# Attention scores taken two levels at a time, a third factor buffer, and a longer stretch of other work behind the state products

## The chip, the cores and the metric

The kernel runs on one NeuronCore of a Trainium2 chip as one program. Its time is the device time of one execution in microseconds (us), lower is better. The names of the engines follow the profile: PE is TensorE (matmuls), PEld its loading of weights, DVE is VectorE, ACT ScalarE, POOL GpSimd, and SP the engine that issues most of the DMAs.

## What is computed

The kernel computes one layer of a hybrid encoder for 1024 tokens of width 1024 with 16 meta tokens ahead of them: a projection, a pooling mixer, a chunked gated linear attention, gates that merge the two, an output projection, and a squared-ReLU MLP. The change lies in the linear attention. For each of 4 heads (64 key and 128 value channels) and each chunk of 64 tokens:

```python
def gla_chunk_step(S, inp):
    qc, kc, vc, ac = inp
    b = jnp.cumsum(ac, axis=2)
    decay = jnp.exp(-jnp.abs(b[:, :, :, None, :] - b[:, :, None, :, :]))
    scores = jnp.einsum('bhtk,bhsk,bhtsk->bhts', qc, kc, decay)
    o = jnp.einsum('bhts,bhsv->bhtv', scores, vc) + jnp.einsum('bhtk,bhkv->bhtv', qc * jnp.exp(b), S)
    b_end = b[:, :, -1:, :]
    S_new = jnp.exp(b_end[:, :, 0, :])[..., None] * S + jnp.einsum('bhsk,bhsv->bhkv', kc * jnp.exp(b_end - b), vc)
    return S_new, o
```

`scores` has a decay of its own for every pair of tokens and channel, so it is no plain product of q and k. The state `S` passes from chunk to chunk.

## The kernel before

Everything is float32, and the large products are done as three matmuls on operands split in a high and a low part (`mm3`, lines 256 to 258). These three lines are by far the most of PE's work. The order of PE is fixed: it executes in the order in which the program is written (`manual_schedule` around the whole drive of the program). On DVE and ACT a scheduler in the build settles the order in the attention stage, out of the order of writing, what each instruction needs, and its own estimates; the engines then execute that order one instruction after the other. Which instruction waits for which is settled by what it reads and writes.

**The attention stage** (`gla`) works through four units: a unit is a pair of heads `p` and a half of the tokens, in the order (0,0), (1,0), (0,1), (1,1). A unit has two generators. `inside(p, half, before)` makes the scores within the chunks; `across(p, half)` handles the state and the output, and runs beside the `inside` of the next unit. In each round of the loop in `gla`, each living generator advances to its next `yield`. Then `pour` issues other work ("filler") on PE: matmuls of the key, value, gate and output projections, which wait in the list `fill`. The number of a `yield` is the length of the stretch to be poured, in us by the kernel's own reckoning, times `PACE` 1.1; the largest of a round counts. What is over or under in one pour is settled in the next. The list `fill` is a fixed amount of work: what isn't poured in a round is poured later.

**`inside`** gets the decays `g` from a small matmul (L1192) and a chain of ACT and DVE operations that ends with an exponential (L1263). Then the scores are built up over a hierarchy. Seven products are taken per unit by `scores`, each a block of 64x64 matmuls (L1249) into one half of the PSUM tile `sc`; the halves take turns. The first block is of plain keys and queries, copied to `scc` by ACT (L1266). The others, levels 0 to 5, use factors in which keys and queries are multiplied by decays, and a masked copy on DVE (L1312) takes from each level the pairs of tokens that belong to it. `grow` makes the factors of the next level from those of this one: DVE multiplies the outer quarters into the new buffer (L1281), ACT copies the inner ones there from the buffer `F` (L1282), DVE multiplies the inner ones in `F` (L1283), and DVE makes the products of decays for the next level, `ends` (L1285). There are two factor buffers, `n0` and `n1`, used by turns. So the factors of a level can only be written when the score block of two levels before has been read. Level 5 is made by `last` (L1294, L1295, L1296), which gives the operands of the state, `kl` and `qe`.

**`across`** transposes `kl` (L1330), takes the products of keys and values (L1338) into the PSUM tile `m2`, and runs the chain of states: eight DVE operations (L1344), each of which needs the one before. Behind a pour of 4.4 come the products of scores and values (L1351), which overwrite the PSUM tile that the chain reads; then a copy of a few elements, `seen` (L1356), after which the products of queries and states (L1361) may add to the same PSUM columns; then the norm of the output (L1370 to L1375), a transposition (L1379), a gate and the split of the result (`yg`, L1386 to L1393).

The rounds of a unit in the steady part are: decays; transposes with the plain score block; L1338 with level 0; L1351 with level 1; L1361 with level 2; then level 3, and L1379 with it or a round later; levels 4 and 5.

The products of weights for the filler are loaded by SP, split by ACT (L83) and by POOL (L87 in this stage), and the filler's results leave PSUM through ACT (L932 to L934, L1074) and DVE (L935, L962, L1157, L1158). `b_mm` and `b_mx` are the three PSUM banks of the filler, used by turns.

Of the kernel before, what the change touches and what calls it, by code (L numbers as in the profile page):

```python
# [8 lines left out]
F32 = mybir.dt.float32  # L9
F32R = mybir.dt.float32r  # L10
U8 = mybir.dt.uint8
ACT = mybir.ActivationFunctionType
ALU = mybir.AluOpType
AX = mybir.AxisListType

P = 128
# [4 lines left out]
HALF = 512  # L21
CH = 64
# [10 lines left out]
PACE, LEVEL = 1.1, 1.6  # L33
# [81 lines left out]
def kernel(  # L115
# [11 lines left out]
    left, right = Stack(tc, "left"), Stack(tc, "right")  # L127
# [895 lines left out]
    def gla_open():  # L1023
        W1.eng = pool
        right.pop_to(1)
        S["N"] = [left.push(f"n{i}", [P, HALF, 2], F32) for i in range(2)]
        S["F"] = left.push("f", [P, HALF, 2], F32)
        banks(keep=1, sc=1, m2=1, mx=1, ms=1)
        rota["mm"] = ("mm", "mm", "mx")
# [12 lines left out]

    def yg_open():
        right.pop_to(0)
        S["yg"] = {h: right.push(f"yg{h}", [P, 2, HEADS, HALF], F32R) for h in (1, 0)}
# [206 lines left out]
    def inside(p, half, before):  # L1252
# [4 lines left out]

        kq = S["kq"][half][:, p, :, OFF[half] : OFF[half] + HALF]
        N, F, scc, g, ends = S["N"], S["F"], S["scc"][:, p], S["g"], S["ends"]
        log_decay(S["lr"], p, HALF, g, S["y"], g)  # L1260
        if (p, half) == (1, 0):
            lr_of(1)
        act.activation(g, g, ACT.Exp, scale=1.0 / TAU)  # L1263
        yield 4.5
        b = scores(kq[:, 0], kq[:, 1])
        act.activation(scc, b, ACT.Copy)  # L1266
        pairs = lambda a: a.rearrange("p (b u) n -> p b u n", u=2)
# [31 lines left out]
        e, at = g, 0  # L1299
        for lvl in range(6):  # L1300
            m, n = 1 << lvl, N[lvl % 2]
            to = at + HALF // (2 * m)
            e2 = ends[:, at:to]
            if lvl < 5:
                grow(m, n, N[1 - lvl % 2], e, e2)
            else:
                while before and before not in done:
                    yield 0.8
                last(n, e, e2)
            e, at = e2, to  # L1310
            b = scores(n[:, :, 0], n[:, :, 1])
            dve.copy_predicated(scc, mask[:, lvl : lvl + 1, None, :].broadcast_to([P, 2, 4, CH]), b)  # L1312
            yield LEVEL

# [4 lines left out]
    def across(p, half):  # L1319
# [23 lines left out]
        for c, dst in enumerate(states[1:]):  # L1343
            dve.scalar_tensor_tensor(dst, states[c], dec[:, c : c + 1], kv[:, c % 2, c // 2], ALU.mult, ALU.add)  # L1344
        yield 4.4

# [8 lines left out]

        dve.tensor_copy(seen, o[:, :, 3, P - 1])  # L1356
        yield 0.8
# [495 lines left out]
```

## Time and profile before

| | |
|---|---|
| runs | 1212.27, 1213.29 and 4245.53 us; the median is 1213.29 us |
| the profiled execution | 1212.85 us, of which its span, from the first to the last instruction, is 1211.0 us |
| PE, share of the span | 98% |
| DVE, share of the span | 72% |
| ACT, share of the span | 51% |
| the attention stage | from about 304 to 470 us of the span |
| granted clock of PE | 0.998 |

One of the three runs is far from the other two; the profiled execution is near those two. "Busy" is the time in which an engine had at least one instruction in work. An instruction group shows its count, its mean duration and the idle time of its engine ahead of it with what ended that idle time. A row of the timeline shows when an instruction started, its duration, and in square brackets the wait ahead of it. On PE matmuls overlap, so the price of a block is read from the starts of the rows around it and not from its duration. A "x32" of the timeline is a block of 16 matmuls of the program, which the profile counts as two each.

### The profile page before, as it was taken

What the parts mean: (1) busy time and instruction counts of PE and PEld (TensorE: products, weight loads), DVE (VectorE), ACT (ScalarE), POOL (GpSimd) and SP (SyncE); (2) the same over time, 40 slices, a digit from 0 to 9 for tenths busy, and PEclk for the clock granted to TensorE, in tenths of its full rate; (3) what the DMA queues carried; (4) which work ended last, traced back from release to release, by engine and by line L of the source; (5) the groups of instructions that cost most, each with busy time, mean ns of one, the idle gap of its engine ahead of it and who ended that gap; (6) DMA issues with size and microseconds to landing.
All of it is one profiled execution on the core that took longest, in us unless ns stands there. A gap on an engine that the chain in (4) does not pass through costs nothing.

```text
span 1211.0 us, 18406 instructions
## 1 busy us (share of the span) xinstructions
PE 1191.4 (98%) x6794; PEld 992.8 (82%) x6794; DVE 874.3 (72%) x1442; ACT 623.3 (51%) x1115; POOL 60.3 (5%) x98
## 2 busy tenths in 40 slices
PE   7999999999999999999999999999999999999997
PEld 7878888898887877888878888888888888888886
DVE  7996677666667878636886767677675887887786
ACT  7667567744546423315655545455454444444554
POOL 2000000000103226000000000000000000000000
PEclk9999999999999999999999999999999999999999
DMA  9043433545107665922254444444479973333532
GB/s 256 2 113 114 121 94 102 154 125 159 40 20 258 196 206 196 327 89 88 87 158 164 152 143 156 146 161 149 153 251 322 348 226 97 98 99 92 174 96 87
DMA packets 144554, 182.24 MB, mean 150 GB/s; under 512 B 10264, under 2 KB 81712, under 8 KB 143952
## 3 DMA queue, kind: packets, MB, share of 16 engines
q1 hardware_dynamic: 143856, 176.81, 45.3%
q0 software_dynamic: 608, 4.26, 1.0%
q8 instruction: 53, 0.87, 0.3%
q14 instruction: 37, 0.30, 0.1%
HBM read 123.36 MB, written 57.67 MB: 149 GB/s over the span
## 4 chain that ended last, share of the span: by engine, by line
PE 87%; DVE 7%; ACT 3%; issue 1%; DMA 1%; POOL 0%; SPq 0%; DVEq 0%; ACTq 0%; POOLq 0%
PE b_mm L256 10%; PE b_mm L258 10%; PE b_mm L257 10%; PE b_ms L257 9%; PE b_ms L258 9%; PE b_ms L256 9%; PE b_x L257 8%; PE b_x L256 8%; PE b_x L258 8%; PE b_sc L1249 1%; PE b_mx L256 1%; PE b_mx L258 1%; PE b_mx L257 1%; DVE w1l L275 1%; DVE ut L787 1%
## 5 line engine op out<-in xcount | busy, mean ns | idle before, releaser
L256 PE MATMUL b_mm<-th,w1h 128*128 128x512 f32 (+1 forms) x308 | 116.2, 377 | 2.0 <-DVE c L822 1.0
L258 PE MATMUL b_mm<-th,w1l 128*128 128x512 f32 (+1 forms) x308 | 114.2, 371 | 0.0
L257 PE MATMUL b_mm<-tl,w1h 128*128 128x512 f32 (+1 forms) x308 | 114.2, 371 | 0.0
L256 PE MATMUL b_x<-th,w1h 128*128 128x512 f32 (+1 forms) x264 | 100.2, 379 | 0.0
L257 PE MATMUL b_x<-tl,w1h 128*128 128x512 f32 (+1 forms) x264 | 100.1, 379 | 0.0
L258 PE MATMUL b_x<-th,w1l 128*128 128x512 f32 (+1 forms) x264 | 99.7, 378 | 0.0
L274 ACT ACTIVATE w1h<-raw 128x512 fp32r<-128x512 f32 x98 | 60.7, 620 | 28.1 <-PE b_ms L257 13.6
L274 ACT ACTIVATE w1h<-fs 128x512 fp32r<-128x512 f32 x78 | 49.0, 630 | 48.1 <-PE b_ms L257 33.9
L275 DVE TENSOR_TENSOR w1l<-raw,w1h 128x512 fp32r<-128x512 f32 x98 | 67.0, 684 | 8.4 <-ACT w1h L274 8.4
L256 PEld LDWEIGHTS b_mm<-th,w1h 128*128 128x128 f32 x308 | 57.8, 188 | 13.6 <-issue 1.9
L258 PEld LDWEIGHTS b_mm<-th,w1l 128*128 128x128 f32 x308 | 57.9, 188 | 10.2
L257 PEld LDWEIGHTS b_mm<-tl,w1h 128*128 128x128 f32 x308 | 57.8, 188 | 9.3
L275 DVE TENSOR_TENSOR w1l<-fs,w1h 128x512 fp32r<-128x512 f32 x78 | 53.3, 686 | 16.3 <-ACT w1h L274 16.2
L274 ACT ACTIVATE w1h<-bt 128x512 fp32r<-128x512 f32 x44 | 27.8, 632 | 66.5 <-issue 62.2
L258 PEld LDWEIGHTS b_x<-th,w1l 128*128 128x128 f32 x264 | 49.7, 188 | 9.5
L256 PEld LDWEIGHTS b_x<-th,w1h 128*128 128x128 f32 x264 | 49.6, 188 | 9.5
L257 PEld LDWEIGHTS b_x<-tl,w1h 128*128 128x128 f32 x264 | 49.6, 188 | 9.2
L1701 DVE TENSOR_TENSOR bt<-w,w 128x512 f32<-128x512 f32 x80 | 54.7, 684 | 2.1 <-DMA w<-in_w_ff_dram 2.1
L274 ACT ACTIVATE fxh<-bt 128x512 fp32r<-128x512 f32 x36 | 22.8, 632 | 56.3 <-issue 50.6
L274 ACT ACTIVATE w1h<-rawx 128x512 fp32r<-128x512 f32 x44 | 27.5, 628 | 45.0 <-PE b_x L257 18.7
L258 PE MATMUL b_ms<-wo,w1l 128*128 128x512 f32 x128 | 49.9, 390 | 0.0
L256 PE MATMUL b_ms<-wo,w1h 128*128 128x512 f32 x128 | 49.8, 389 | 0.0
(447 smaller groups left out, 3331.8 us busy)
## 6 DMA issues: line engine op xcount, KB each, us to landing
hf_dram<-h SPq DMA_DIRECT2D x112, 256.0 KB, 2.1
raw<-hf_dram SPq DMA_DIRECT2D x112, 256.0 KB, 2.7
w<-in_w_ff_dram SPq DMA_DIRECT2D x64, 256.0 KB, 4.7
raw<-in_w_in_dram SPq DMA_DIRECT2D x22, 512.0 KB, 4.3
raw<-in_w_ff_dram SPq DMA_DIRECT2D x16, 512.0 KB, 4.2
rawx<-in_w_ff_dram SPq DMA_DIRECT2D x16, 512.0 KB, 4.1
rawx<-in_w_in_dram SPq DMA_DIRECT2D x10, 512.0 KB, 4.3
xs<-in_x_dram SPq DMA_DIRECT2D x8, 512.0 KB, 5.5
```

Source lines behind the costliest of these rows:

```text
L256: pe.matmul(ps, ah, bh, start=first and i == 0, stop=False, skip_group_check=more)
L257: pe.matmul(ps, ah, bl, start=False, stop=False, skip_group_check=more)
L258: pe.matmul(ps, al, bh, start=False, stop=last and i == n - 1, skip_group_check=more)
L274: act.activation(hi, a, ACT.Copy)
L275: dve.tensor_tensor(lo, a, f32(hi), ALU.subtract)
L787: dve.tensor_tensor(to_, a_, b_, ALU.subtract)
L1249: pe.matmul(b[to, e, j], kk[r, s], qq[r, s], start=True, stop=True, tile_position=(e * CH, u * CH))
L1701: dve.tensor_tensor(bt, w, S["w2"][q[3:]][:, i], ALU.add if q[2] == "+" else ALU.subtract)
```

## The change

Three things change in the attention stage; nothing is computed otherwise.

1. **Pairs of levels and a third factor buffer.** The factors rotate over three buffers. In the first unit the third is a new tile `n2`; in later units it lies over the keys and queries of the first unit, `kq0`, which are no longer needed. The seven score blocks of a unit are issued as (plain, level 0), (level 1, level 2), (level 3, level 4) and (level 5), with the two blocks of a pair directly behind each other on PE. The factors of level 1 are made before the first pair's blocks are written, those of level 2 behind them; those of levels 3 and 4 behind the second pair; those of level 5 behind the third. The plain block moves from the round of the transposes to that of the products of keys and values.
2. **Order on DVE.** The making of the factors of levels 3 and 4 is ordered behind the last operation of the chain of states. In the built order, the chain now stands together, with one masked copy in it.
3. **`across`.** The pour behind the chain of states is 5.4 instead of 4.4, except for the last unit. The copy `seen` goes from DVE to ACT.

```diff
--- before.py
+++ after.py
@@ -1,4 +1,4 @@
-from contextlib import ExitStack
+from contextlib import ExitStack, nullcontext
 from itertools import chain
 
 import concourse.bass as bass
@@ -1025,6 +1025,8 @@
         right.pop_to(1)
         S["N"] = [left.push(f"n{i}", [P, HALF, 2], F32) for i in range(2)]
         S["F"] = left.push("f", [P, HALF, 2], F32)
+        S["left_n2"] = left.mark()
+        S["N"].append(left.push("n2", [P, HALF, 2], F32))
         banks(keep=1, sc=1, m2=1, mx=1, ms=1)
         rota["mm"] = ("mm", "mm", "mx")
 
@@ -1041,6 +1043,8 @@
             leave()
 
     def yg_open():
+        assert S["unit"] != (0, 0)
+        left.pop_to(S["left_n2"])
         right.pop_to(0)
         S["yg"] = {h: right.push(f"yg{h}", [P, 2, HEADS, HALF], F32R) for h in (1, 0)}
 
@@ -1256,14 +1260,15 @@
 
 
         kq = S["kq"][half][:, p, :, OFF[half] : OFF[half] + HALF]
+        S["unit"] = p, half
         N, F, scc, g, ends = S["N"], S["F"], S["scc"][:, p], S["g"], S["ends"]
+        if (p, half) != (0, 0):
+            N[2] = S["kq"][0][:, 0].rearrange("p a b -> p (a b)")[:, : 2 * HALF].rearrange("p (t n) -> p t n", n=2)
         log_decay(S["lr"], p, HALF, g, S["y"], g)
         if (p, half) == (1, 0):
             lr_of(1)
         act.activation(g, g, ACT.Exp, scale=1.0 / TAU)
         yield 4.5
-        b = scores(kq[:, 0], kq[:, 1])
-        act.activation(scc, b, ACT.Copy)
         pairs = lambda a: a.rearrange("p (b u) n -> p b u n", u=2)
         plain, gp = kq.rearrange("p n (b u) -> p b u n", u=2), g.rearrange("p (b u) -> p b u", u=2)
         for u, to, other in ((1, N[0], F), (0, F, N[0])):
@@ -1297,20 +1302,38 @@
 
         yield 2.0
         e, at = g, 0
-        for lvl in range(6):
-            m, n = 1 << lvl, N[lvl % 2]
-            to = at + HALF // (2 * m)
-            e2 = ends[:, at:to]
-            if lvl < 5:
-                grow(m, n, N[1 - lvl % 2], e, e2)
-            else:
+
+        def up(lvl):
+            nonlocal e, at
+            to = at + HALF // (2 << lvl)
+            (grow if lvl < 5 else last)(*level(lvl), e, ends[:, at:to])
+            e, at = ends[:, at:to], to
+
+        def level(lvl):
+            return (1 << lvl, N[lvl % 3], N[(lvl + 1) % 3]) if lvl < 5 else (N[lvl % 3],)
+
+        def masked(lvl, b):
+            dve.copy_predicated(scc, mask[:, lvl : lvl + 1, None, :].broadcast_to([P, 2, 4, CH]), b)
+
+        up(0)
+        for pair in ((None, 0), (1, 2), (3, 4), (5,)):
+            if pair == (5,):
                 while before and before not in done:
                     yield 0.8
-                last(n, e, e2)
-            e, at = e2, to
-            b = scores(n[:, :, 0], n[:, :, 1])
-            dve.copy_predicated(scc, mask[:, lvl : lvl + 1, None, :].broadcast_to([P, 2, 4, CH]), b)
-            yield LEVEL
+                up(5)
+            made = []
+            for lvl in pair:
+                n = kq.rearrange("p n t -> p t n") if lvl is None else N[lvl % 3]
+                made.append((lvl, scores(n[:, :, 0], n[:, :, 1])))
+            with tc.issue_after(S["chain"].ins) if "chain" in S and pair[-1] == 2 else nullcontext():
+                for lvl in {0: (1,), 2: (2, 3), 4: (4,)}.get(pair[-1], ()):
+                    up(lvl)
+            for lvl, b in made:
+                if lvl is None:
+                    act.activation(scc, b, ACT.Copy)
+                else:
+                    masked(lvl, b)
+            yield len(pair) * LEVEL
 
     rms = [tiny(8) for _ in range(2)]
     seen = tiny(2)
@@ -1341,8 +1364,10 @@
                 )
         states = [first] + [W[:, c] for c in range(NC - 1)] + ([S["S"][:, 1, p]] if half == 0 else [])
         for c, dst in enumerate(states[1:]):
-            dve.scalar_tensor_tensor(dst, states[c], dec[:, c : c + 1], kv[:, c % 2, c // 2], ALU.mult, ALU.add)
-        yield 4.4
+            S["chain"] = dve.scalar_tensor_tensor(
+                dst, states[c], dec[:, c : c + 1], kv[:, c % 2, c // 2], ALU.mult, ALU.add
+            )
+        yield 4.4 if (p, half) == (1, 1) else 5.4
 
         o = two("m2").rearrange("p e (j c) -> p e j c", j=4)
         for j in range(4):
@@ -1353,7 +1378,7 @@
                         tile_position=(u * CH, (u ^ e) * CH), skip_group_check=True,
                     )
 
-        dve.tensor_copy(seen, o[:, :, 3, P - 1])
+        act.activation(seen, o[:, :, 3, P - 1], ACT.Copy)
         yield 0.8
         for j in (3, 0, 1, 2):
             for e, u in ((0, 0), (1, 0), (1, 1), (0, 1)):
```

On PE in unit (0,1), before: the products of scores and values with the block of level 1 behind them, and filler around them (`b_m2` is the PSUM tile of the state and output products, `b_sc` that of the scores, `n1` a factor buffer).

```order
L258 MATMUL b_mm_3875<-th1_140,w1l_128 128x512
L1351 MATMUL b_m2_3888<-v1_2690,scc_2715 64x128 x16
L1249 MATMUL b_sc_2951<-n1_2847 64x64 x16
L256 MATMUL b_mx_3930<-th1_140,w1h_124 128x512
L257 MATMUL b_mx_3930<-tl1_144,w1h_124 128x512
```

The same place in the changed kernel; `kq0` is now the third factor buffer and holds level 2.

```order
L258 MATMUL b_mx_3900<-th1_140,w1l_128 128x512
L1376 MATMUL b_m2_3913<-v1_2690,scc_2715 64x128 x16
L1253 MATMUL b_sc_2976<-n1_2847 64x64 x16
L1253 MATMUL b_sc_2976<-kq0_2234 64x64 x16
L256 MATMUL b_mm_3976<-th1_140,w1h_124 128x512
```

The block of level 2 stood behind a stretch of filler and the products of queries and states; it now follows the block of level 1 directly.

On DVE in unit (0,1), before: the chain of states (`W`, at the end `S`), the masked copy of level 0 into `scc`, and the multiplications that make the factors of level 2 (`n0`, `f`), then two operations of the filler.

```order
L1344 SCALAR_TENSOR_TENSOR W_2723<-S_2719,ends_2706,b_m2_3806 128x128
L1344 SCALAR_TENSOR_TENSOR W_2723<-W_2723,ends_2706,b_m2_3806 128x128 x2
L1312 COPY_PREDICATED scc_2715<-mask_91,b_sc_2951 128x512
L1344 SCALAR_TENSOR_TENSOR W_2723<-W_2723,ends_2706,b_m2_3806 128x128
L1281 TENSOR_TENSOR n0_2843<-n1_2847,ends_2706 128x64x2x4
L1344 SCALAR_TENSOR_TENSOR W_2723<-W_2723,ends_2706,b_m2_3806 128x128
L1283 TENSOR_TENSOR f_2851<-n1_2847,ends_2706 128x64x8
L1344 SCALAR_TENSOR_TENSOR W_2723<-W_2723,ends_2706,b_m2_3806 128x128 x2
L1344 SCALAR_TENSOR_TENSOR S_2719<-W_2723,ends_2706,b_m2_3806 128x128
L1296 TENSOR_TENSOR ends_2706<-ends_2706 128x8
L935 SCALAR_TENSOR_TENSOR t1_2694<-b_mm_3763,t1_2694 128x512
```

In the changed kernel, the same place begins with the factors of level 2, which go to `kq0`; then the chain, then the factors of level 3 in `n0`.

```order
L1286 TENSOR_TENSOR kq0_2234<-n1_2847,ends_2706 128x64x2x4
L1290 TENSOR_TENSOR ends_2706<-ends_2706 128x128
L1288 TENSOR_TENSOR f_2851<-n1_2847,ends_2706 128x64x8
L1367 SCALAR_TENSOR_TENSOR W_2723<-S_2719,ends_2706,b_m2_3800 128x128
L1367 SCALAR_TENSOR_TENSOR W_2723<-W_2723,ends_2706,b_m2_3800 128x128 x6
L1316 COPY_PREDICATED scc_2715<-mask_91,b_sc_2976 128x512
L1367 SCALAR_TENSOR_TENSOR S_2719<-W_2723,ends_2706,b_m2_3800 128x128
L1286 TENSOR_TENSOR n0_2843<-kq0_2234,ends_2706 128x32x2x8
L1290 TENSOR_TENSOR ends_2706<-ends_2706 128x64
L1290 TENSOR_TENSOR ends_2706<-ends_2706 128x32
L1288 TENSOR_TENSOR f_2851<-kq0_2234,ends_2706 128x32x16
```

The two multiplications that stood in the midst of the chain now stand ahead of it, and those behind it are of the next level.

On ACT in unit (0,1), before: the last part of a filler's gate (`t1`, `o`), the copy of inner factors, the square of the output for its norm.

```order
L932 ACTIVATE t1_2694<-b_mm_3763 128x512
L933 ACTIVATE t1_2694<-t1_2694 128x512
L934 ACTIVATE t1_2694<-t1_2694 128x512
L1074 ACTIVATE o_2698<-t1_2694 128x512
L1282 ACTIVATE n1_2847<-f_2851 128x32x16
L1370 ACTIVATE mix_2702<-b_m2_3888 128x1024
```

In the changed kernel, the same place holds the copy `seen` (to `small`), which reads the output products in `b_m2`.

```order
L1287 ACTIVATE n0_2843<-f_2851 128x32x16
L933 ACTIVATE t1_2694<-t1_2694 128x512
L934 ACTIVATE t1_2694<-t1_2694 128x512
L1078 ACTIVATE o_2698<-t1_2694 128x512
L1381 ACTIVATE small_99<-b_m2_3913 128x2
L1287 ACTIVATE n1_2847<-f_2851 128x16x32
```

The copy stands behind the gate of the filler and ahead of two copies of factors.

## The prediction

> **What bounds the kernel now.** I read the busy shares first, then the stage that the change touches, then what PE waits for there, then single blocks.
>
> ```profile
> PE 1191.4 (98%) x6794; PEld 992.8 (82%) x6794; DVE 874.3 (72%) x1442; ACT 623.3 (51%) x1115; POOL 60.3 (5%) x98
> PE 87%; DVE 7%; ACT 3%; issue 1%; DMA 1%; POOL 0%; SPq 0%; DVEq 0%; ACTq 0%; POOLq 0%
> ```
>
> PE sets the time: it is busy 98% of the span, and 87% of the chain that ended last is PE. In the attention stage, by windows (columns: PE, PEld, DVE, ACT, POOL busy, granted clock, DMA share, GB/s) and by waits of PE:
>
> ```profile
> 300.00:470.00 170.00, 167.44 (x2012) 138.63 (x2011) 118.75 (x244) 76.85 (x137) 38.15 (x48) 1.00 0.47 159
> PE b_m L1351 <- DVE S L1344: 0.7, 1, 0.7
> PE b_sc L1249 <- DVE scc L1312: 0.7, 1, 0.7
> PE b_m L1351 <- DVE W L1344: 0.5, 1, 0.5
> PE b_m L1379 <- DVE mix L1375: 0.4, 1, 0.4
> PE b_mx L256 <- DVE t L1157: 0.2, 1, 0.2
> ```
>
> PE is idle for 2.56 of 170 us, at full clock; the named waits are 2.3 us for operations that the change moves and 0.2 us for L1157, which it does not. The built order is the same from the last unit's products on and before the stage, on PE, DVE and ACT. So two things can be gained: these waits, and time in which PE is "busy" with changing over between kinds of matmul.
>
> **The price of a change-over.** On PE, a score block alone in the filler (columns: start, duration, engine, line, operation, count):
>
> ```profile
> 317.15 0.40 PE L258 MATMUL b_mm<-th,w1l 128*128 128x512 f32 x1
> 317.48 0.71 PE L1249 MATMUL b_sc<-n 64*64 64x64 f32 x32
> 318.12 0.50 PE L256 MATMUL b_mm<-th,w1h 128*128 128x512 f32 x1
> 318.45 0.39 PE L257 MATMUL b_mm<-tl,w1h 128*128 128x512 f32 x1
> 318.68 0.39 PE L258 MATMUL b_mm<-th,w1l 128*128 128x512 f32 x1
> ```
>
> Undisturbed filler starts every 0.23 us (318.45 to 318.68). From 317.15 to 318.45 there are 1.30 us with two filler matmuls, 0.46. The block alone costs **0.84 us**. Behind a product that uses the same 64x64 tiles:
>
> ```profile
> 452.80 1.10 PE L1338 MATMUL b_m<-v,mix 64*64 64x128 f32 x32
> 453.83 0.50 PE L256 MATMUL b_mm<-yg,w1h 128*128 128x512 f32 x1
> ...
> 418.51 1.10 PE L1338 MATMUL b_m<-v,mix 64*64 64x128 f32 x32
> 419.43 0.66 PE L1249 MATMUL b_sc<-n 64*64 64x64 f32 x32
> 420.02 0.50 PE L256 MATMUL b_mm<-th,w1h 128*128 128x512 f32 x1
> ```
>
> The product alone holds the filler back by 1.03 us, with a block behind it by 1.51. The block costs **0.48 us** there. Behind the transposes, which use the whole array, it gains nothing:
>
> ```profile
> 450.18 0.60 PE L1330 MATMUL b_ms<-ident,mix 128*128 128x128 f32 x4
> 450.53 0.48 PE L256 MATMUL b_mm<-yg,w1h 128*128 128x512 f32 x1
> ...
> 375.96 0.60 PE L1330 MATMUL b_ms<-ident,mix 128*128 128x128 f32 x4
> 376.49 0.69 PE L1249 MATMUL b_sc<-kq 64*64 64x64 f32 x32
> 377.11 0.50 PE L256 MATMUL b_mm<-th,w1h 128*128 128x512 f32 x1
> ```
>
> 1.15 less 0.35 is 0.80 us, nearly the price of a block alone.
>
> **The change, part by part.** *Pairs.* Before, seven blocks of unit (0,0) stand alone, and in each later unit four: the plain one, level 3 (with the transposes L1379 or alone), 4 and 5. That is 19 at 0.84 and 9 at 0.48. After, unit (0,0) has four groups; in later units each of three pairs follows a 64x64 product, and level 5 follows the transposes. That leaves 4 + 3 = 7 blocks that pay the change-over, and 21 that don't. Twelve blocks, the second ones of the pairs, go from 0.84 to a lower price. No row shows a block behind another block. The lower bound of its price is 0.48, from the block behind a product; the upper is 0.64, the time from 317.48 to 318.12 that a lone block holds the filler back behind its own start. I take 0.48, since that row too is 64x64 behind 64x64. **12 x 0.36 = 4.3 us less**, or 12 x 0.20 = 2.4 with 0.64.
>
> [...]
>
> *Waits behind the chain of states.* On DVE in unit (0,1), where the wait of 0.7 us is:
>
> ```profile
> 377.39 0.69 DVE L1281 TENSOR_TENSOR n<-n,mix 128x512 f32<-128x512 f32 x1
> 377.99 0.97 DVE L1285 TENSOR_TENSOR ends<-mix 128x256 f32<-128x256 f32 x1
> 378.99 2.27 DVE L1285 TENSOR_TENSOR ends<-ends 128x128 f32<-128x128 f32 x4
> 381.17 0.68 DVE L935 SCALAR_TENSOR_TENSOR t<-b_mx,t 128x512 f32<-128x512 f32 x1
> 381.77 0.68 DVE L1283 TENSOR_TENSOR f<-n,mix 128x512 f32<-128x512 f32 x1
> 382.37 0.34 DVE L1344 SCALAR_TENSOR_TENSOR W<-S,ends,b_m 128x128 f32<-128x128 f32 x1
> 382.75 0.73 DVE L1344 SCALAR_TENSOR_TENSOR W<-W,ends,b_m 128x128 f32<-128x128 f32 x2
> 383.40 0.73 DVE L1312 COPY_PREDICATED scc<-mask,b_sc 128x512 f32<-128x512 uint8 x1
> 384.02 0.33 DVE L1344 SCALAR_TENSOR_TENSOR W<-W,ends,b_m 128x128 f32<-128x128 f32 x1
> 384.27 0.68 DVE L1281 TENSOR_TENSOR n<-n,ends 128x512 f32<-128x512 f32 x1
> ...
> 386.94 0.35 DVE L1344 SCALAR_TENSOR_TENSOR S<-W,ends,b_m 128x128 f32<-128x128 f32 x1
> ```
>
> The chain takes 4.9 us, from 382.37 to 387.29. Standing together it needs 8 x 0.38 (382.37 to 382.75) and one masked copy of 0.62 (383.40 to 384.02): 3.7 us. But two multiplications, 1.2 us at 0.6 from start to start (381.77 to 382.37), move ahead of it. Three of the small `ends` move behind it, at least 0.7 us. So it ends about 0.7 us earlier against the decays. In this unit ACT's order puts a load's split (L83, 1.05 us) ahead of the exponential that all this waits for, so the end may come 0.3 later instead. PE comes later to the products: the longer pour adds 1.1 us, two blocks at 0.48 stand where one stood, the plain block's 0.80 is gone ahead, and three filler matmuls (0.7) more stand ahead of the transposes. That is about 1.5 us. Both waits for the chain, 0.7 and 0.5, should go; what is next there is PE itself.
>
> *Waits for the norm and a masked copy*, 0.4 and 0.7, both in unit (1,1). In the rounds around L1375, two multiplications for factors and one or two operations of the filler no longer stand between the reduction (L1373) and L1375; one masked copy more does. The norm comes earlier by 2 x 0.6 - 0.62 = 0.6 us at least, and the level-4 block asked for earlier no longer waits there. I take all four waits as gone: **2.3 us less**; the bounds are nothing and 2.3.
>
> *What is now asked for earlier.* Level 2 is wanted a round earlier, level 4 two rounds. In unit (0,1) DVE has, from the end of the chain to the masked copy that frees the level-4 block's half of `sc`, five multiplications at 0.6, two masked copies at 0.62, four `ends` at about 0.2, and three filler operations at 0.6 (L935, 381.17 to 381.77): 6.8 us. PE needs 1.03 + 2 x 0.48 for the products and blocks, 3.5 for the pour, 1.03 and 0.48 until that block, 7.0 us, and the chain ends about a microsecond before it. The slack is a microsecond. Against it: where POOL is in work, these multiplications are slower.
>
> ```profile
> 414.91 3.99 POOL L87 TENSOR_TENSOR w1l<-raw,w1h 128x256 fp32r<-128x256 f32 x4 [11.47 <-ACT w1h L83]
> L1281 DVE TENSOR_TENSOR n<-n,mix x4: 673/686/1215, 311.7 to 416.2; 128x512 f32<-128x512 f32 x4
> ```
>
> The one of 1215 ns (minimum 673, median 686) started at 416.2, within POOL's 414.91 to 418.90: 0.53 us more. I add **0.6 us** of new waits, between nothing and 3 us (six such slow operations).
>
> *The copy `seen`* costs PE nothing unless it comes behind the pour. On ACT it stands behind a filler gate and ahead of two copies. After the pairs PE pours 3.5 us before it is needed; only in the last unit is the pour 0.9 us. A small operation on ACT takes 0.30 us:
>
> ```profile
> 394.71 0.30 ACT L220 ACTIVATE small<-small 128x8 f32<-128x8 f32 x1 [0.77 <-DVE small L1373]
> ```
>
> So it is hidden, with half a microsecond of slack in the last unit; if the cover is gone, it costs these 0.3 us a unit. *The filler* is the same in count, and the same work stands behind the last chain in both orders. The pours of a later unit sum to 4.5 + 2 + 5.4 + 3.2 + 6 + 1.6 = 22.7 against 23.3, so no unit is stretched. DMAs and the queues of SP and POOL change only in interleaving.
>
> **Sum.** 1212.85 (profiled execution) - 4.3 - 2.3 + 0.6 = 1206.9; with the rounding of rows, **1207 us**, half a per cent under the median of 1213.29. About 2% is what a measurement of this kernel can tell from no change, so this counts as no change.
>
> **The rivals.**
>
> *The second block of a pair costs nearly as much* (0.64), and half of the waits come back in other places: 1212.85 - 2.4 - 1.2 + 0.6 = 1209.9. For it: the lone block's own 0.64 is what is seen most. Against: the three places behind products show 0.48.
>
> *The waits hide other waits, and PE's order gains nothing*: the change does not do what it says, 1213. For it: PE is idle only 1.5% of the stage, and 98% busy all over. Against: the change-over is within busy time, and 0.36 us is measured.
>
> *Level 4 comes too late, and the time ends above before.* The place is the third pair in units (1,0), (0,1), (1,1). The ten multiplications of a unit up to there run while POOL splits weights; at 0.53 us each that is 5.3 us a unit, less a slack of 1 us in (0,1) and, as an estimate, 2.6 in each of the others, where the chain ends earlier or DVE has less of the filler: 3 x 5.3 - 6.2 = 9.7 us of waits, and 1212.85 - 6.6 + 9.7 = 1216. It decides from 6.6 us of new waits, 2.2 a unit. Against: POOL's block is 4 us long, so that few of the ten fall in one, and the unit in which it lies paid no more than the wait of 0.5 for the chain. [...]
>
> **How the numbers follow.** Forecast 64%, the dear second block 20%, no gain 6%, late level 4 10%. The forecast's own bounds are 1205.8 (all gains, no new wait) and 1209.5 (3 us of new waits); the second rival reaches to 1211. The range 1205.6 to 1212.0 leaves out the no-gain and the late case and little else. None of the cases comes near 2%, which is 24 us; 1% faster, 97% within, 2% slower is for stalls that no row here hints at.
>
> **What would show it.** The pairs on PE: the second block's start to the next filler at about 0.5. Idle of PE in the stage under 1 us, with no wait of L1376 (then the line of L1351) for the chain. DVE's chain in one piece of 3.7 us. Wrong would be: waits of the score blocks for `f`, `n` or `scc` in the third pair, a wait of L1386 for ACT's copy, or filler waiting for a bank because L935 is late.

## The result, and the profile after

The changed kernel takes **1205.88 us**, the median of six runs (1204.46 to 1206.74). The kernel before, measured with it, takes 1212.8 us, the median of six runs, or 1212.4 without the one run of 4245.53 us that stands far from the others. The ratio of the others is 0.9944, with a 95% interval from 0.9934 to 0.9954: nearly seven microseconds, half a per cent. The profiled execution is the slowest of the six, 1206.74 us, with a span of 1205.0 us.

The page of the changed kernel, engines and chain (the lines that answer to the first two of the prediction):

```profile
PE 1186.7 (98%) x6794; PEld 992.4 (82%) x6794; DVE 874.9 (73%) x1438; ACT 623.9 (52%) x1119; POOL 60.2 (5%) x98
PE 89%; DVE 5%; ACT 2%; DMA 2%; issue 1%; POOL 0%; SPq 0%; DVEq 0%; POOLq 0%; ACTq 0%
```

PE has the same 6794 instructions, and its busy time is 4.7 us less. The attention stage can be cut out exactly: it begins with the first matmul of the decays and ends with the first filler matmul behind it that goes to `b_x`; so it ends at 477.6 us in the kernel before, not at about 470. From the timeline and the windows of the kernel before:

```profile
304.21 0.17 PE L1192 MATMUL b_mm<-lrT_meta,wgu 80*128 80x16 f32 x1
477.58 0.39 PE L256 MATMUL b_x<-yg,w1h 128*128 128x512 f32 x1
304.21:477.58 173.37, 170.81 (x2029) 141.55 (x2028) 125.48 (x252) 78.83 (x141) 43.69 (x53) 1.00 0.48 159
```

The same stretch of the changed kernel:

```profile
304.66 0.17 PE L1196 MATMUL b_mm<-lrT_meta,wgu 80*128 80x16 f32 x1
472.08 0.39 PE L256 MATMUL b_x<-yg,w1h 128*128 128x512 f32 x1
304.66:472.08 167.42, 166.04 (x2029) 140.71 (x2028) 125.72 (x247) 79.37 (x144) 43.60 (x53) 1.00 0.50 165
```

In both windows PE has 2029 matmuls, so this is the same work. The stage is 5.95 us shorter: busy time fell by 4.77 us, from 170.81 to 166.04, and idle time by 1.18 us, from 2.56 to 1.38. The two profiled executions differ by 6.11 us (1212.85 to 1206.74), so nearly all of the gain lies in this stage.

What PE waits for in the stage of the changed kernel:

```profile
PE b_m L1386 <- ACT small L1381: 1.2, 1, 1.2
PE b_mx L256 <- DVE t L1161: 0.2, 1, 0.2
```

The four waits of before (0.7, 0.7, 0.5 and 0.4 us) are gone. There is one new wait, of the last unit's products of queries and states (L1386, formerly L1361) for the copy `seen` (L1381, formerly L1356).

A pair of blocks on PE, behind the products of keys and values of unit (0,1):

```profile
378.65 0.40 PE L258 MATMUL b_mm<-th,w1l 128*128 128x512 f32 x1
378.98 1.10 PE L1361 MATMUL b_m<-v,mix 64*64 64x128 f32 x32
379.90 0.64 PE L1253 MATMUL b_sc<-kq 64*64 64x64 f32 x32
380.37 0.66 PE L1253 MATMUL b_sc<-n 64*64 64x64 f32 x32
380.96 0.50 PE L256 MATMUL b_mm<-th,w1h 128*128 128x512 f32 x1
```

The product and two blocks hold the filler back by 1.98 us, from 378.98 to 380.96. Before, the product with one block took 1.51. The second block costs **0.47 us**, where a block alone cost 0.84.

The chain of states on DVE in the same unit:

```profile
382.27 0.34 DVE L1367 SCALAR_TENSOR_TENSOR W<-S,ends,b_m 128x128 f32<-128x128 f32 x1
382.64 2.27 DVE L1367 SCALAR_TENSOR_TENSOR W<-W,ends,b_m 128x128 f32<-128x128 f32 x6
384.82 0.74 DVE L1316 COPY_PREDICATED scc<-mask,b_sc 128x512 f32<-128x512 uint8 x1
385.45 0.33 DVE L1367 SCALAR_TENSOR_TENSOR S<-W,ends,b_m 128x128 f32<-128x128 f32 x1
387.32 1.10 PE L1376 MATMUL b_m<-v,scc 64*64 64x128 f32 x32
```

It stands in one piece with one masked copy in it, from 382.27 to 385.78, which is 3.5 us instead of 4.9. PE pours until 387.32, when L1376 (formerly L1351) starts: the chain is 1.5 us early.

**Where the new wait comes from.** From SP's issues to PE, in the last unit of the changed kernel (SPq rows: when a DMA was issued):

```profile
444.80 0.38 SPq L963 DMA_DIRECT2D ma_dram<-o  x1
451.64 0.79 SPq L1095 DMA_DIRECT2D o<-ma_dram  x2
454.48 0.69 DVE L1162 TENSOR_TENSOR t<-t,o 128x512 f32<-128x512 f32 x1 [0.52 <-DMA o<-ma_dram]
455.20 0.63 ACT L1165 ACTIVATE th<-t 128x512 fp32r<-128x512 f32 x1 [2.86 <-DVE t L1162]
455.74 0.15 ACT L1381 ACTIVATE small<-b_m 128x2 f32<-128x2 f32 x1
455.95 0.45 PE L1386 MATMUL b_m<-W,mix 64*64 64x128 f32 x8 [1.18 <-ACT small L1381]
```

The copy itself takes 0.15 us. Ahead of it on ACT stands the split of the merged results (L1165), which waits for DVE's sum (L1162), which waits for a load that was issued only at 451.64. SP had been held there:

```profile
SPq L1095 <- DMA ma_dram<-o: 7.6, 2, 4.5
```

The load goes into a slot of `o`, of which there are three. By this row SP waited until an earlier result had left its slot on the way to `ma_dram`.

### The profile page after: what moved, and what is told of

Read it like the earlier page. It is cut to its first block, busy times and chain, and to the rows that moved or that the text cites. A ratio compares the mean times of both kernels' runs of the same rounds, so it can differ in the third digit from the quotient of the medians.

```text
span 1205.0 us, 18370 instructions
## 1 busy us (share of the span) xinstructions
PE 1186.7 (98%) x6794; PEld 992.4 (82%) x6794; DVE 874.9 (73%) x1438; ACT 623.9 (52%) x1119; POOL 60.2 (5%) x98
## 4 chain that ended last, share of the span: by engine, by line
PE 89%; DVE 5%; ACT 2%; DMA 2%; issue 1%; POOL 0%; SPq 0%; DVEq 0%; POOLq 0%; ACTq 0%
PE b_mm L256 10%; PE b_mm L258 10%; PE b_mm L257 10%; PE b_ms L258 10%; PE b_ms L257 10%; PE b_ms L256 10%; PE b_x L257 8%; PE b_x L256 8%; PE b_x L258 8%; PE b_sc L1253 1%; PE b_mx L256 1%; DMA ma_dram<-o 1%; PE b_mx L258 1%; PE b_mx L257 1%; DVE ut L787 1%
```

## Experiments

The theory was the prediction's: blocks in pairs save 0.36 us each, and the longer pour and the order on DVE keep the waits away. The rivals were that the busy time went for another reason, that the waits would have gone without these parts, and, once the trace was seen, that the parts around the pairs work through the late load of the last unit. The ratios are to the kernel before, which was run beside each series and had medians of 1212.6 to 1212.9 us; where a time is set against the 1205.88 us of the changed kernel, that is across series.

### The pairs split up

```diff
             for lvl in pair:
+                if len(pair) > len(made):
+                    S["pour"](0.65)
...
-            yield len(pair) * LEVEL
+            yield len(pair) * LEVEL - 0.59 * (len(pair) - 1)
```

Three or six filler matmuls stand between the two blocks of each pair; the rest is the changed kernel.

> The changed kernel with one short stretch of filler (three or six matmuls) between the two blocks of each pair, taken from the pour behind the pair; everything else as changed. Theory (the gain is the change-over of PE between filler and 64x64 blocks): each of 12 second blocks costs 0.84 instead of 0.48 us, so 1205.9 + 4.3 = 1210.2 us, with PE's waits as in the changed kernel. Rival (the gain comes from the waits that went, or from the times at which factors are made): 1205.5 to 1206.5 us. Third, if a block drains the array whatever stands ahead of it: no change either, and the second blocks show the same price in both.

Measured: 1213.96 us (1213.49 to 1216.24), ratio to the kernel before 1.001, interval 1.0001 to 1.0019. All of the gain is gone. PE in unit (0,1), and the stage:

```profile
385.26 0.64 PE L1253 MATMUL b_sc<-kq 64*64 64x64 f32 x32
385.83 0.50 PE L256 MATMUL b_mm<-th,w1h 128*128 128x512 f32 x1
386.17 0.39 PE L257 MATMUL b_mm<-tl,w1h 128*128 128x512 f32 x1
386.39 0.40 PE L258 MATMUL b_mm<-th,w1l 128*128 128x512 f32 x1
386.72 0.71 PE L1253 MATMUL b_sc<-n 64*64 64x64 f32 x32
387.36 0.50 PE L256 MATMUL b_mm<-th,w1h 128*128 128x512 f32 x1
387.70 0.40 PE L257 MATMUL b_mm<-tl,w1h 128*128 128x512 f32 x1
304.82:478.87 174.05, 171.26 (x2029) 141.13 (x2028) 127.29 (x248) 79.83 (x145) 44.78 (x55) 1.00 0.48 158
```

From 386.39 to 387.70 there are 1.31 us with two filler matmuls of 0.23; the second block costs 0.85 us again, with only three filler matmuls in front of it. The same 2029 matmuls are busy for 171.26 us, 5.22 more than with the pairs. Idle time is 1.41 us more; one wait of 1.4 us for POOL's split (L87) is new and was not expected. So the busy time is the pairs', and the expectation of 1210.2 was too low: 12 pairs are worth 5.2 us here and 4.8 in the comparison with before, 0.40 to 0.44 us each, somewhat more than the 0.37 that the rows of one pair show.

### The copy `seen` back on DVE

```diff
-        act.activation(seen, o[:, :, 3, P - 1], ACT.Copy)
+        dve.tensor_copy(seen, o[:, :, 3, P - 1])
```

> The changed kernel with the copy `seen` back on DVE. In the changed profile L1386 waits 1.2 us for it in the last unit, and nowhere else. Theory A (ACT's queue is at fault: the copy stands behind another instruction there): the wait goes, 1204.7 us. Theory B (a load of the output merge lands late, and the DVE operation that needs it, L1162, stands ahead of the copy on DVE as well): a wait of 0.6 to 0.9 us stays, for DVE, and the time is 1205.2 to 1205.6 us.

Measured: 1205.36 us (1204.87 to 1206.82), ratio 0.9941, interval 0.9929 to 0.9953: not to be told from the changed kernel. The time lies in theory B's range, but the trace is theory A's: PE's wait at L1386 is gone from the stage, which leaves only the 0.2 us for L1161. In the MLP, PE waits 1.4 us in two places for DVE (L1664), where the profiled execution of the changed kernel has no such wait, and the spans are the same 1205.0 us. The part "`seen` on ACT" is worth nothing that these runs can tell.

### A longer pour in the last unit

```diff
-        yield 0.8
+        yield 2.2 if (p, half) == (1, 1) else 0.8
```

> The changed kernel with a pour of 2.2 instead of 0.8 between the copy `seen` and L1386, in the last unit alone. If the copy's lateness is all that holds PE there, six to seven filler matmuls cover the 1.2 us, and the time is 1204.7 us with no wait at L1386. Rival: the filler behind the norm is then short by as much, and the 1.2 us come back as a wait of L1404 or of the filler for its loads; 1205.9 us.

Measured: 1207.72 us (1205.72 to 1210.28), ratio 0.9959, interval 0.9946 to 0.9971; neither expected time held. The five runs are far apart, and the profiled execution, 1209.55 us, is one of the slower. In it the wait at L1386 went, and another came at the transposes of the output, the place that the rival named, with a lower clock behind it:

```profile
466.49 1.80 PE L1404 MATMUL b_m<-ident,mix 128*128 128x128 f32 x8 [2.26 <-DVE mix L1400]
464.00:468.00 4.00, 1.74 (x10) 1.51 (x9) 3.76 (x8) 0.21 (x1) 0.68 (x1) 0.84 0.64 201
468.00:472.00 4.00, 4.00 (x15) 3.24 (x14) 3.93 (x7) 2.29 (x4) 3.50 (x4) 0.73 0.37 79
```

The filler is a fixed amount: what is poured ahead of L1386 is missing ahead of L1404.

### The pairs alone, and the third part alone

The pairs alone: the changed kernel without the order on DVE, with the pour of 4.4 and `seen` on DVE.

```diff
-            with tc.issue_after(S["chain"].ins) if "chain" in S and pair[-1] == 2 else nullcontext():
+            with nullcontext():
...
-        yield 4.4 if (p, half) == (1, 1) else 5.4
+        yield 4.4
...
-        act.activation(seen, o[:, :, 3, P - 1], ACT.Copy)
+        dve.tensor_copy(seen, o[:, :, 3, P - 1])
```

> Only the pairs and the third buffer: no order behind the chain on DVE, pour 4.4, `seen` on DVE. Theory (pairs carry the change-over, the other two parts only the waits of L1376 for the chain): PE's blocks as in the changed kernel, the waits for the norm and the masked copy gone, but waits of up to 1 us in two or three units for the chain, so 1206 to 1208.5 us. Rival (order and pour are what makes the pairs possible): waits of several us for the chain and for factors, 1210 us or more.

Measured: 1211.81 us (1210.53 to 1212.73), ratio 0.999, interval 0.9981 to 0.9999. The time is in the rival's range: the pairs alone keep 1.1 of the seven microseconds. Two long waits of PE, and the clock behind the first and the second of them:

```profile
386.75 1.10 PE L1376 MATMUL b_m<-v,scc 64*64 64x128 f32 x32 [2.53 <-DVE S L1367]
388.00:392.00 4.00, 4.00 (x66) 3.40 (x60) 3.50 (x8) 1.47 (x3) 0.00 (x0) 0.60 0.90 295
457.62 0.45 PE L1386 MATMUL b_m<-W,mix 64*64 64x128 f32 x8 [2.56 <-DVE small L1381]
460.00:464.00 4.00, 4.00 (x19) 3.30 (x18) 3.30 (x8) 0.54 (x3) 0.00 (x0) 1.00 1.02 366
```

The stage takes 173.17 us, as long as before, of which PE is idle for 5.26 and busy for 167.91. What the pairs save, PE now waits: it comes to the same DVE results earlier.

The third part alone, on the kernel before (the second, the order on DVE, was not tried there):

```diff
-        yield 4.4
+        yield 4.4 if (p, half) == (1, 1) else 5.4
...
-        dve.tensor_copy(seen, o[:, :, 3, P - 1])
+        act.activation(seen, o[:, :, 3, P - 1], ACT.Copy)
```

> The kernel before with the third part alone: pour 5.4 behind the chain of states, `seen` on ACT; two buffers, no pairs. Theory (pour removes only the two waits of L1351 for the chain, 0.7 and 0.5): 1211.5 to 1212.0 us, those two waits gone, the waits for the norm and the masked copy as before or moved, perhaps 1 us for `seen` in the last unit, then 1212.5 us. Rival (the longer pour is what won the 7 us): 1207 to 1209 us.

Measured: 1217.16 us (1215.55 to 1217.43), ratio 1.0031, interval 1.0019 to 1.0044: slower, outside both expectations. Its waits in the stage:

```profile
PE b_m L1361 <- ACT small L1356: 2.5, 1, 2.5
PE b_sc L1249 <- DVE scc L1312: 1.5, 2, 0.8
```

The two waits for the chain went, as the theory has it. But PE waits 2.5 us for the copy in the last unit: on ACT it stands behind a split of weights (L83) that waits 3.79 us for its load, while DVE has nothing to do at that time. PE's waits for masked copies are 1.5 us instead of 0.7, and the granted clock behind the long wait was 0.81 from 470 to 475 us. The stage is 3.9 us longer than before, half of it in waits and half in busy time. So neither the pairs nor the third part brings the gain by itself: 1.1 us and -4.4 us apart, 6.9 us with all three parts together.

### Order, pour and buffer taken away one at a time

Without the order on DVE (`nullcontext()` as above, nothing else):

> The changed kernel without the order of the factors behind the chain; pour 5.4 and `seen` on ACT as changed. In the kernel with pairs only, a multiplication of 1.24 us and another of 0.77 stood in the chain in unit (0,1), and PE waited 2.5 us for it. Theory (the longer pour alone covers that, 1.2 us of it, the order the rest): a wait of L1376 of 0.5 to 1.5 us in one unit; 1206.5 to 1208 us. Rival (the order is not needed once the pour is longer): 1205.5 to 1206.3 us.

Measured: 1206.93 us (1205.95 to 1207.79), ratio 0.9951, interval 0.9937 to 0.9966. The interval overlaps with that of the changed kernel. The time is in the theory's range, but the wait for the chain that the theory rests on did not come: PE's waits in the stage are the same two as in the changed kernel, 1.1 and 0.2 us, as the rival has it. With the longer pour in place, the order is worth about one microsecond, which is not clear of noise, and the trace of the stage doesn't show where it would come from.

With the pour of 4.4 everywhere (`yield 4.4`, nothing else):

> The changed kernel with the pour of 4.4 in all units; the order and `seen` on ACT as changed. Theory: the chain stands together and ends 1 to 1.5 us earlier than without the order, so a wait of L1376 of about 1 us is left in unit (0,1), and the filler left over stands behind the last unit, where it costs nothing; 1206.5 to 1208 us. Rival (order alone does): 1205.5 to 1206.3 us.

Measured: 1211.72 us (1209.13 to 1215.04), ratio 0.999, interval 0.9979 to 1.0. The pour decides over 5.8 us, much more than either expectation. The ten runs are far apart: the three with a clock of 0.998 or 0.999 over the whole span took 1209.1 to 1210.7 us, the four with 0.995 or 0.996 took 1211.9 to 1215.0. The waits, what PE and DVE do ahead of the second, and the clock behind it:

```profile
385.68 1.10 PE L1376 MATMUL b_m<-v,scc 64*64 64x128 f32 x32 [0.93 <-DVE S L1367]
449.78 1.10 PE L1376 MATMUL b_m<-v,scc 64*64 64x128 f32 x32
454.13 0.69 DVE L1162 TENSOR_TENSOR t<-t,o 128x512 f32<-128x512 f32 x1 [1.45 <-DMA o<-ma_dram]
455.60 0.71 PE L1386 MATMUL b_m<-W,mix 64*64 64x128 f32 x8 [3.11 <-ACT small L1381]
456.00:460.00 4.00, 4.00 (x38) 3.19 (x31) 1.22 (x1) 1.51 (x2) 0.97 (x2) 0.50 1.04 369
460.00:464.00 4.00, 4.00 (x15) 3.15 (x14) 3.33 (x9) 0.51 (x2) 0.00 (x0) 0.76 0.45 152
304.91:477.62 172.71, 168.67 (x2030) 143.03 (x2028) 125.12 (x249) 79.39 (x145) 42.93 (x54) 0.98 0.49 160
```

The chain of states, for which the pour was made longer, costs 0.93 us. The larger part is the wait of 3.11 us in the last unit, whose own pour isn't changed, and 2.6 us of busy time at the lower clock (168.67 against 166.04). With less filler in the three units ahead, PE comes to the last unit's L1376 at 449.78 us instead of 452.06; but DVE's sum, which needs the late load, starts at 454.13, hardly earlier than the 454.48 of the changed kernel. So the longer pours also cover that load.

With two factor buffers instead of three:

```diff
-            return (1 << lvl, N[lvl % 3], N[(lvl + 1) % 3]) if lvl < 5 else (N[lvl % 3],)
+            return (1 << lvl, N[lvl % 2], N[(lvl + 1) % 2]) if lvl < 5 else (N[lvl % 2],)
...
-                n = kq.rearrange("p n t -> p t n") if lvl is None else N[lvl % 3]
+                n = kq.rearrange("p n t -> p t n") if lvl is None else N[lvl % 2]
```

> The changed kernel with two factor buffers by turns; pairs, order, pour and `seen` as changed. The factors of level 2 then wait for the block of level 0 to be read, those of level 3 for level 1 and those of level 4 for level 2, all of the pair before, which is issued a whole round ahead of its use. Theory A (the third buffer lets the factors of level 2 be made ahead of the chain, and without it they come behind or delay the chain): waits of 1 to 3 us in each later unit, 1208 to 1213 us. Theory B (the pour covers it): 1205.5 to 1207 us.

Measured: 1208.88 us (1207.65 to 1209.82), ratio 0.9967, interval 0.9954 to 0.998. With two buffers the kernel is about 3 us slower. The time is in theory A's range, but its waits in each later unit did not come: in unit (0,1) two multiplications for factors do stand in the chain of states again (L1286 at 383.90, L1288 at 384.76), and PE doesn't wait for it. PE waits 0.4 us at a score block and 2.0 us at L1386 in the last unit, where DVE waits 2.9 us for a load (`t` from `gb_dram`). Its stage is 1.35 us longer than that of the changed kernel, and most of that is the late loads again and not the buffers themselves.

### A slot of its own for the last outgoing result

The last wait was tested by taking away what the trace says the load waits for: the last of the pool's results goes to `ma_dram` from columns of `kq0` that are free by then, so the load finds a slot that no outgoing write holds.

```diff
-                o = nxt("o")
+                o = S["kq"][0][:, 1, 0, :HALF] if (j, e, h) == (3, 1, 1) else nxt("o")
```

On the changed kernel:

> The changed kernel, with one edit: the last result that the pool writes to ma_dram is put into free columns of kq instead of a slot of o, so that the load that follows takes a slot that no outgoing write holds. Nothing is left out of the computation. Theory: the 1.2 us wait of TensorE for ScalarE's copy in the last unit comes from that slot, since the load in front of the merge is issued only once the write has landed; with a spare slot the wait goes and the time is about 1204.7 us. Rival: the write isn't what holds the load, the wait stays, and the time is that of the changed kernel, 1205.9 us.

Measured: 1206.38 us (1206.06 to 1207.49), ratio 0.9952, interval 0.994 to 0.9965. The load and PE in the last unit, the stage, and two places in the MLP:

```profile
447.76 1.36 SPq L1095 DMA_DIRECT2D o<-ma_dram  x1
455.16 0.45 PE L1386 MATMUL b_m<-W,mix 64*64 64x128 f32 x8 [0.40 <-ACT small L1381]
304.66:471.28 166.62, 166.04 (x2029) 140.72 (x2028) 125.50 (x248) 79.38 (x145) 44.04 (x53) 1.00 0.50 166
611.29 0.47 PE L256 MATMUL b_mm<-th,w1h 128*128 128x512 f32 x1 [0.64 <-DVE h L1664]
889.80 0.47 PE L256 MATMUL b_mm<-th,w1h 128*128 128x512 f32 x1 [0.83 <-DVE h L1664]
```

The load is issued at 447.76 instead of 451.64, DVE's sum no longer waits for it, and PE waits 0.40 us instead of 1.18; what is left is another load (`t` from `gb_dram`), for which DVE waits 1.1 us at L1161. The stage is 0.80 us shorter at the same busy time. So the outgoing write was what held the load, and two thirds of PE's wait come from it. But the time isn't lower: the profiled execution pays 1.5 us at two places of the MLP where the changed kernel's paid nothing. The same places took 1.4 us with `seen` on DVE. This repeats: in the traces of the four kernels with pairs in which the last unit waits less (`seen` on DVE, and the spare slot here and in the next two), what follows the stage takes 734.1 to 735.5 us, with 1.1 to 1.6 us of these waits; in the ten other traces it takes 732.5 to 733.4, with 0.8 us of them at most. Why these waits take back what the last unit gains is not settled.

On the changed kernel with the pour of 4.4:

> The changed kernel with the old pour of 4.4 and the spare slot for the last pool result. Nothing is left out of the computation. Theory: with the pour of 4.4 most of the 5.8 us came from the 3.1 us wait of the last unit and the lower clock behind it, both from the late load; with the spare slot they go, the 0.9 us wait for the state chain stays, and the time is 1206.5 to 1207.5 us. Rival: the shorter pour itself costs it, at the state chain, and the time stays near 1211.7 us.

Measured: 1209.01 us (1208.23 to 1210.81), ratio 0.9972, interval 0.9962 to 0.9983, between the two expectations. PE's wait at L1386 is 1.26 us instead of 3.11, the wait of 0.92 for the chain stays, and the clock is 1.00 in the windows behind both (388 to 392 and 456 to 460 us):

```profile
304.57:473.09 168.52, 166.16 (x2030) 140.51 (x2028) 124.69 (x247) 78.73 (x144) 42.87 (x53) 1.00 0.49 161
```

The stage is 4.19 us shorter than without the slot, but the time only 2.7, since part of it is lost again behind the stage. So of the 5.8 us that the shorter pour costs, 2.7 go with the late load.

On the pairs alone:

> The paired products alone (old order of the factors, pour of 4.4, copy of seen on VectorE) with the spare slot. Nothing is left out of the computation. Theory: the 2.6 us wait for the copy of seen goes, the 2.5 us wait for the state chain and the lower clock behind it stay, and the time is 1208 to 1209.5 us. Rival: the load isn't what was late, and the time stays at 1211.8 us.

Measured: 1210.74 us (1208.96 to 1211.66), ratio 0.9984, interval 0.9975 to 0.9993: 1.1 us less than without the slot, and outside the range expected. Its stage is 169.62 us, 3.55 us shorter than that of the pairs alone, but its span is only 1.2 us shorter (1210.8 to 1209.6). Some 2.2 us were lost again behind the stage; 1.4 of them stand in waits of PE, for L1664 in the MLP (1.6 against 0.6 us) and for the split of the output projection's weights (L1499, 0.4). The wait for the chain and the clock behind it:

```profile
386.89 1.10 PE L1376 MATMUL b_m<-v,scc 64*64 64x128 f32 x32 [2.52 <-DVE S L1367]
388.00:392.00 4.00, 4.00 (x78) 3.39 (x70) 3.83 (x8) 1.62 (x3) 0.00 (x0) 1.00 0.94 289
```

On the kernel before:

> The kernel before with the spare slot alone. Nothing is left out of the computation. Theory: TensorE of the kernel before doesn't wait for the copy of seen, so the slot costs it nothing, and the time is that of the kernel before, 1212.8 us within 0.5 us. Rival: the late load costs the kernel before as well, and the time falls by 1 us or more.

Measured: 1213.19 us (1212.86 to 1213.86), ratio 1.0005, interval 0.9996 to 1.0014. As the theory has it, the slot is worth nothing where PE doesn't come to the copy early.

None of these versions can be told to beat the changed kernel.

## Why the prediction was right, point by point

The forecast was 1207.0 us, the time 1205.88; for the profiled execution 1206.9 against 1206.74. The direction and the main term held; two of its terms were off in opposite directions. By its own terms the lower bound is 1212.85 - 4.3 - 2.3 = 1206.25 us and the upper, with 3 us of new waits, 1209.25, not 1205.8 and 1209.5; the median of 1205.88 lies below that lower bound, the profiled execution within.

- *The price of a change-over.* Shown. The second block of a pair costs 0.47 us by the rows, where 0.48 was taken and 0.64 was the upper bound, and 0.85 again as soon as filler stands between.
- *"12 x 0.36 = 4.3 us less."* The mechanism is right, the size is off by half a microsecond: busy time fell by 4.77 us at the same 2029 matmuls. The rows of the kernel before account for nearly all of it. With 0.47 in place of 0.48 the twelve blocks give 4.4 us. Three of the lone blocks cost more than the one at 317.48, which starts 0.33 us behind the filler matmul ahead of it: those at 367.99 and 403.64 start 0.40 us behind theirs, and the one at 356.44 starts 0.49 us behind a small product (L1231) that another block follows by 0.36. That adds 0.3 us.
- *The four waits, 2.3 us less.* They are gone. For the chain, the prediction put its end 0.7 us earlier against the decays and PE 1.5 us later, which, less the wait of 0.7, leaves 1.5 us to spare. Counted from the first multiplication behind the decays (375.93 us before, 375.59 after), the chain ends 1.2 us earlier and PE comes 1.0 us later, and the chain is 1.5 us early: the two terms were off in opposite directions, their sum was about right. PE doesn't wait for the chain even in the run without the order on DVE.
- *"0.6 us of new waits", at the third pair for level 4.* The size was near and the place was wrong. No score block waits, although most multiplications beside POOL were slower, as assumed: those of `n` by `mix` took 954 ns in the median and 1217 at most. Of the forty that make factors (L1286, L1288), the seven that took 0.79 to 1.23 us all started while POOL split weights (L87); two more that started then, and the other 31, took 0.67 to 0.70. It is not so each time: in the kernel before, five that started then took 0.86 to 1.23 us, and two, at 434.49 and 435.71, took 0.68 within POOL's 433.10 to 436.98. The new wait is 1.18 us, and it lies elsewhere.
- *The copy `seen`, "hidden, with half a microsecond of slack in the last unit".* **This step failed.** PE waits 1.18 us for the copy. The price was taken from a small operation on ACT alone. What counts is what stands ahead of it in ACT's queue: the merge of filler results, which waits for DVE, which waits for a load, which waits for an outgoing write. The prediction named a wait of L1386 for ACT's copy among the signs of being wrong, and it came.
- *"DMAs and the queues of SP and POOL change only in interleaving."* True of the count, and wrong as a reason to leave them out: 0.78 of the last 1.18 us went when the load no longer had to be issued as late as 451.64.
- *The pours, "no unit is stretched".* No wait in the stage speaks against it. Not seen was how much hangs on them: 1.1 us of pour in three units are worth 5.8 us, of which the chain explains 0.9 us in the profile; the late load of the last unit, which the pours cover as well, explains 2.7.
- *The rivals.* A dear second block falls by the 0.47. "No gain" did not come for the change as a whole, but its mechanism, waits that hide behind other waits, is what the runs with the pour of 4.4 show: 1211.8 us with the pairs alone, and 1211.7 with everything but the longer pours. The late level 4 did not come; its mechanism, the slower multiplications beside POOL, was there without a wait at a score block.

In the stage the sum was -4.3 - 2.3 + 0.6 = -6.0 us and the trace has -5.95: busy time gave 0.5 more, and waits 0.5 less. That the total came out so near is partly this cancellation.

## What to carry to other kernels

Here it was worth putting the blocks of small matmuls next to each other on TensorE: a block of 16 cost 0.84 us alone in the filler and 0.47 directly behind another, 0.37 less. But an engine that is made faster comes earlier to everything that it waits for, so such a change has to bring its own cover with it; here the pairs kept 1 us without the longer pours, and 7 with them. The cover need not stand where the wait is: filler poured in earlier units made PE come to the last unit's L1376 at 452.06 us instead of 449.78, and so later to a load there. When a small operation is moved to another engine, follow the queue ahead of it down to the DMAs, not only its own duration.

## What was not expected of the hardware

Behind waits of TensorE of 2.3 to 3.1 us the granted clock was lower for some microseconds in four places, and full in two. Behind 2.26 us (the longer pour in the last unit) the clock of the next window of 4 us was 0.73, behind 3.11 us (the pour of 4.4) 0.50 and then 0.76, behind 2.53 us (the pairs alone) 0.60, behind 2.54 us (the third part alone) 0.81 in a window of 5 us. Behind 2.56 us in the execution of the pairs alone it was 1.00, and at the same place as the 0.60, after 2.52 us, it was 1.00 in the run with the spare slot. Behind the 1.18 us of the changed kernel, the 1.43 us with the pairs split and the 2.04 us with two buffers it was 1.00. Where it falls, it adds to the wait: busy time is 2.5 us more with the pour of 4.4 (168.67 against 166.16 with the spare slot), and 1.6 with the pairs alone (167.91 against 166.34).

One window lies wholly in the lower clock, 456 to 460 us with the pour of 4.4, and shows 0.50. If the clock is 0.50 for as long as it is low, its duration can be estimated from the windows: what a window's clock lacks to 1.00, times the window's length, over 0.50, summed:

| wait of PE (us) | run | its end (us) | clock in the windows from there | lower clock, estimate (us) |
|---|---|---|---|---|
| 3.11 | pour of 4.4 | 455.60 | 0.89 (452 to 456), 0.50 (456 to 460), 0.76 (460 to 464) | 6.8 |
| 2.56 | pairs alone, second | 457.62 | 1.00 (456 to 460), 1.00 (460 to 464) | none |
| 2.54 | third part alone | 467.52 | 0.85 (465 to 470), 0.81 (470 to 475) | 3.4 |
| 2.53 | pairs alone, first | 386.75 | 0.97 (384 to 388), 0.60 (388 to 392) | 3.4 |
| 2.52 | pairs alone, spare slot | 386.89 | 1.00 (384 to 388), 1.00 (388 to 392) | none |
| 2.26 | longer last pour | 466.49 | 0.84 (464 to 468), 0.73 (468 to 472) | 3.4 |
| 2.04 | two buffers | 457.47 | 1.00 (456 to 460), 1.00 (460 to 464) | none |

In the four cases with a lower clock the next window shows 1.00 again. The length of the wait alone doesn't tell the cases apart: 2.26 and 2.53 us were followed by the lower clock, 2.52 and 2.56 us were not. What decides was not shown by these runs.
